# Latent attention: queries, keys and maxima from 4-byte pairs to scaled fp16 pairs

## The chip, the cores and the metric

The kernel runs on one core of a Trainium2 chip. The time is the device time of one execution in microseconds (us). Three runs were made, and their median is the time that counts.

## The reference

One encoder layer over 2048 tokens of width 1024: a first LayerNorm, a projection `w_in`, three groups of attention heads, a gate on each group's normalised output, an output projection and a closing LayerNorm. The change touches the second group, the latent attention of 8 heads. Cut to that:

```python
q = (_rms_norm(c_q, g_cq, dt) @ w_uq).reshape(b, s, MLA_HEADS, 64 + 32)
q_nope, q_rope = q[..., :64], _rope(q[..., 64:], pos)
kv = (_rms_norm(c_kv, g_ckv, dt) @ w_ukv).reshape(b, s, MLA_HEADS, 64 + 64)
k_nope, v = kv[..., :64], kv[..., 64:]
k_rope = _rope(b_kr[:, :, None, :], pos)[:, :, 0]          # one for all heads
sc = (einsum('bqhe,bkhe->bhqk', q_nope, k_nope)
      + einsum('bqhr,bkr->bhqk', q_rope, k_rope)) * 96 ** -0.5
o = einsum('bhqk,bkhe->bqhe', softmax(sc, axis=-1), v)
```

## The kernel before

**Split operands.** Products are made from a high and a low part of each operand: high by high, high by low and low by high, summed in PSUM. In the input projection both parts are fp16, scaled by a power of two that is worked out from the weights' norms (`Block.scale`, `root_power`). In the latent attention they are 4-byte parts in TensorE's fp32r form, without a scale (`R(...)` marks an operand so).

**Where the latent operands come from.** The last block of the projection, B_C + 3, gives the shared rotary key: in four chunks of 512 tokens it is scaled, turned and stored as `krh_d` and `krl_d` (lines 1160 to 1180). Then the pool `up` opens. `all_weights` loads `w_uq` in three pieces and `w_ukv` in two, and splits each on ScalarE and GpSimd; the first piece of `w_ukv` holds the keys, the second the values. The up-projection itself is cut into small steps (`up_chunk`: load, queries, rope, values, turn, keys), which stand in the list `fill`. The gate blocks 10 to 12 are projected meanwhile, and between two of their eight-part sums `paced(20, 1.4)` takes steps from `fill`: none in the first 20 calls (two and a half gate chunks), then 1.4 per call. `split_store` makes the two parts of 512 queries or keys, on ScalarE and VectorE (GpSimd for the rotary part), and stores them to `mqh_d`, `mql_d`, `mrh_d`, `mrl_d`, `mkh_d`, `mkl_d`. Its buffers, tags `uh` and `ul`, are also those of the raw weights.

**Order.** From the memory keys on, TensorE's instructions run in the order of the program (`in_order()`), while a planner orders the other engines and the DMA queue. From the dilated attention on, all engines run in the program's order (`in_order(*EALL)`).

**The latent attention.** A `Head` loads the four tiles `qh`, `ql`, `kh`, `kl` (96 rows of 2048) of its head, while the head before is worked on. Row 96 of `kh` is a constant and row 96 of `qh` holds the negated maximum of each query's scores, so that the first of the three products subtracts it. The maxima are made ahead, two steps per unit: a product of the high parts (`product`, line 1451), a reduction on VectorE (line 1457), and for each 512 queries a turn through TensorE and a conversion on ScalarE (`max_turn`, lines 1463 to 1468), whose result a DMA brings to row 96. A unit is 512 queries against 256 keys: six score matmuls (lines 1503 to 1505), two exponentials of the same 1024 columns on ScalarE (`probabilities`: `pf` in fp32, line 1349, and `ph` in fp16, line 1360), their difference `pl` on VectorE or, each third time, GpSimd (line 1363), and later 24 value matmuls (lines 1528 to 1530). `push_two` runs units in pairs: scores of both, then the value matmuls of two earlier units. The bias of the exponentials is `shift_t`, 4 ln 2. The dilated attention before it uses the same `probabilities` with a scale from a tile, `ascale`.

## Time and profile before

| | us |
|---|---|
| median of three runs | 2882.62 |
| lowest and highest | 2881.8, 2887.9 |
| the profiled execution, its own time | 2884.62 |
| its span in the profile | 2882.9 |
| TensorE busy | 2713.0 (94%) |
| VectorE busy | 1959.8 (68%) |
| ScalarE busy | 1547.0 (54%) |
| GpSimd busy | 929.1 (32%) |

In the profile PE is TensorE's matmul, PEld its weight load, DVE is VectorE, ACT ScalarE, POOL GpSimd and SP the engine that issues the DMAs; L12 is line 12 of the kernel. Matmuls are pipelined: a matmul's duration runs to the modelled end of its results, and the next starts before that. The profiled execution's own time is 1.7 us over its span.

### The profile page before, as it was taken

What the parts mean: (1) busy time and instruction counts of PE and PEld (TensorE: products, weight loads), DVE (VectorE), ACT (ScalarE), POOL (GpSimd) and SP (SyncE); (2) the same over time, 40 slices, a digit from 0 to 9 for tenths busy, and PEclk for the clock granted to TensorE, in tenths of its full rate; (3) what the DMA queues carried; (4) which work ended last, traced back from release to release, by engine and by line L of the source; (5) the groups of instructions that cost most, each with busy time, mean ns of one, the idle gap of its engine ahead of it and who ended that gap; (6) DMA issues with size and microseconds to landing.
All of it is one profiled execution on the core that took longest, in us unless ns stands there. A gap on an engine that the chain in (4) does not pass through costs nothing. (4 is left out here: it accounts for less than half of the span.)

```text
span 2882.9 us, 56842 instructions
## 1 busy us (share of the span) xinstructions
PE 2713.0 (94%) x22618; PEld 1893.3 (66%) x22665; DVE 1959.8 (68%) x4483; ACT 1547.0 (54%) x2071; POOL 929.1 (32%) x628
## 2 busy tenths in 40 slices
PE   6999999999999999899888888999999999899998
PEld 5544445544546774454777776888888877778887
DVE  7433344469982776543788887777777778688886
ACT  7644435532124665342788885878887767422221
POOL 3101013433232001212777773333333335222221
PEclk9999999999999999999999999999999999999999
DMA  5434346653224112686578596312323312556662
GB/s 179 140 102 131 97 143 152 167 154 102 83 79 150 54 54 93 204 276 213 149 167 209 155 185 138 75 33 75 82 66 68 70 41 64 158 167 176 180 181 90
DMA packets 279337, 367.53 MB, mean 127 GB/s; under 512 B 38304, under 2 KB 198176, under 8 KB 274976
## 3 DMA queue, kind: packets, MB, share of 16 engines
q1 hardware_dynamic: 279072, 363.90, 46.3%
q8 instruction: 178, 2.92, 0.4%
q14 instruction: 87, 0.71, 0.1%
HBM read 225.57 MB, written 138.20 MB: 126 GB/s over the span
## 5 line engine op out<-in xcount | busy, mean ns | idle before, releaser
L181 PE MATMUL ps_mm<-hT,w_h 128*128 128x512 f16 x2944 | 879.3, 381 | 4.6 <-ACT w_h L338 4.6
L181 PE MATMUL ps_mm<-hT,w_l 128*128 128x512 f16 x1472 | 558.0, 380 | 0.4 <-DVE w_l L342 0.4
L181 PEld LDWEIGHTS <-w_h 128*128 128x128 f16 x2944 | 277.2, 99 | 283.4 <-issue 20.5
L1363 POOL TENSOR_TENSOR pl<-pf,ph 128x1024 f16<-128x1024 f32 x117 | 297.7, 2544 | 465.1 <-ACT ph L1360 306.4
L1457 DVE TENSOR_REDUCE lmc<-ps_x 128x1 f32<-128x512 f32 x496 | 319.2, 685 | 143.1 <-PE ps_x L1451 142.6
L1349 ACT ACTIVATE pf<-ps_s,shift_t 128x1024 f32<-128x1024 f32 x256 | 285.5, 1115 | 138.1 <-PE ps_s L1505 134.3
L1363 DVE TENSOR_TENSOR pl<-pf,ph 128x1024 f16<-128x1024 f32 x217 | 292.4, 1348 | 7.3 <-ACT ph L1360 6.2
L1360 ACT ACTIVATE ph<-ps_s,shift_t 128x1024 f16<-128x1024 f32 x254 | 282.7, 1113 | 0.0
L181 PEld LDWEIGHTS <-w_l 128*128 128x128 f16 x1472 | 144.5, 98 | 175.3 <-DVE w_l L342 1.5
L1349 ACT ACTIVATE pf<-ps_s,shift_t,ascale 128x1024 f32<-128x1024 f32 x160 | 192.7, 1204 | 83.2 <-PE ps_s L1701 46.9
L1503 PE MATMUL ps_s<-hq,hq 97*128 97x512 f32 x512 | 218.7, 427 | 13.4 <-DMA hq<-lmr 11.2
L1528 PEld LDWEIGHTS <-ph 128*128 128x128 f16 x2032 | 187.4, 97 | 33.6 <-issue 33.1
L1530 PE MATMUL ps_o<-lv,pl 128*128 128x65 f16 x2032 | 202.1, 193 | 3.7 <-POOL pl L1363 3.7
L1504 PE MATMUL ps_s<-hq,hq 96*128 96x512 f32 x512 | 205.0, 400 | 0.0
L1528 PE MATMUL ps_o<-lv,ph 128*128 128x65 f16 x2032 | 204.1, 194 | 0.0
L1505 PE MATMUL ps_s<-hq,hq 96*128 96x512 f32 x512 | 203.6, 398 | 0.0
L1529 PE MATMUL ps_o<-lv,ph 128*128 128x64 f16 x2032 | 202.9, 196 | 0.0
L1530 PEld LDWEIGHTS <-pl 128*128 128x128 f16 x2032 | 189.3, 100 | 4.1 <-POOL pl L1363 3.8
L1529 PEld LDWEIGHTS <-ph 128*128 128x128 f16 x2032 | 189.4, 98 | 0.0
L1701 PE MATMUL ps_s<-hq,hq 128*128 128x256 f16 (+3 forms) x1536 | 185.6, 258 | 2.8 <-issue 0.2
L880 DVE CUSTOM_DVE_ANT_0 d1j<-ps_x,wm 128x256 bf16<-128x256 f32 (+1 forms) x608 | 184.7, 364 | 1.6 <-PE ps_x L877 0.8
L1701 PEld LDWEIGHTS <-hq 128*128 128x128 f16 (+1 forms) x1536 | 149.4, 120 | 39.5 <-issue 10.5
(379 smaller groups left out, 6086.4 us busy)
## 6 DMA issues: line engine op xcount, KB each, us to landing
w_raw<-in_w_in_dram SPq DMA_DIRECT2D x56, 512.0 KB
oa<-oa_d SPq DMA_DIRECT2D x48, 520.0 KB
v<-va_d SPq DMA_DIRECT2D x24, 1032.0 KB
oa_d<-so SPq DMA_DIRECT2D x16, 1040.0 KB
gate_d<-sg SPq DMA_DIRECT2D x64, 256.0 KB
lv<-gate_d SPq DMA_DIRECT2D x15, 1024.0 KB
wo_raw<-in_w_out_dram SPq DMA_DIRECT2D x26, 512.0 KB
hq<-k_n SPq DMA_DIRECT2D x16, 576.0 KB
```

What stands on the lines that cost most here:

```text
L181: nc.tensor.matmul(ps, R(a), R(b), start=(i == 0), stop=(i == n - 1))
L1349: nc.scalar.activation(pf, ps, AF.Exp, bias=shift_t, scale=scale)
L1360: nc.scalar.activation(ph, ps, AF.Exp, bias=shift_t, scale=scale)
L1363: pipe.later.append(lambda: lo_engine.tensor_tensor(out=pl, in0=pf, in1=ph, op=ALU.subtract))
L1457: nc.vector.tensor_reduce(out=self.mc[:, t % 4, n:n + 1], in_=ps, axis=AX.X, op=ALU.max)
L1503: nc.tensor.matmul(b, R(cur.kh[0:97, kc]), R(cur.qh[0:97, c]), start=True, stop=False)
L1504: nc.tensor.matmul(b, R(cur.kh[0:96, kc]), R(cur.ql[0:96, c]), start=False, stop=False)
L1505: nc.tensor.matmul(b, R(cur.kl[0:96, kc]), R(cur.qh[0:96, c]), start=False, stop=True)
L1528: nc.tensor.matmul(o, ph, v[:, 0:65], start=(k2 == 0 and j == 0 and i == 0), stop=False, skip_group_check=True)
L1529: nc.tensor.matmul(o[:, 0:64], ph, v[:, 65:129], start=False, stop=False, skip_group_check=True)
L1530: nc.tensor.matmul(o, pl, v[:, 0:65], start=False, stop=(k2 == 7 and j == 1 and i == 3), skip_group_check=True)
L1701: nc.tensor.matmul(o, kt[:, key], q, start=(i in bare and kt is ks and first), stop=(kt is kk and c0 == 512), skip_group_check=True)
```

## The change

The latent queries, keys, rotary keys and negated maxima become fp16, in the scratch memory and on the chip (`head_set(..., F16)` for both sets). To fit them into fp16's range, powers of two are worked out on the chip from the norms of the gain-weighted up-projection weights: `squares_of` sums squares of the raw weights on ScalarE, and `latent_powers` adds them over the partitions with a matmul and takes roots and products on VectorE. The queries and keys are multiplied by their power as they are split; the rotary key is left in its block's scale. The exponent's scale undoes the powers, from a tile, and the shift of 4 ln 2 moves from the exponential's bias into the row of maxima. `split_store` has buffers of its own. `root_power` can guard against zero.

```diff
-    mqh_d = scratch("mqh_d", [BH, 64, S])
+    mqh_d = scratch("mqh_d", [BH, 64, S], F16)
...
+    lpow = cpool.tile([P, 3], F32, name="lpow")
+    lscale = cpool.tile([P, 2], F32, name="lscale")
+    krinv = cpool.tile([P, 1], F32, name="krinv")
...
-        def root_power(dst, src):
-
-            y = wpool.tile([P, 1], F32, tag="rp", name="rp")
+        def root_power(dst, src, guard=False):
+
+            y = wpool.tile([P, src.shape[-1]], F32, tag="rp", name="rp")
+            if guard:
+                nc.vector.tensor_scalar(out=y, in0=src, scalar1=1e-20, scalar2=None, op0=ALU.max)
+                src = y[:]
             nc.vector.tensor_scalar(out=y.bitcast(I32), in0=src.bitcast(I32), scalar1=-0.5, scalar2=float(0x5F3759DF + (14 << 23)),
...
-                root_power(self.ws[:], ps[:, 8:9])
+                root_power(self.ws[:], ps[:, 8:9], self.b == B_C + 3)
...
-                nc.vector.tensor_tensor(out=sg, in0=sg, in1=w.un, op=ALU.mult)
+
+                nc.vector.tensor_scalar(out=sg, in0=sg, scalar1=2.0 ** -14, scalar2=None, op0=ALU.mult)
+                nc.vector.tensor_scalar(out=krinv, in0=w.un, scalar1=2.0 ** 14, scalar2=None, op0=ALU.mult)
...
-                    nc.vector.scalar_tensor_tensor(out=t1, in0=ps[0:32, :], scalar=w.un[0:32, :], in1=tb[0][0:32, :], op0=ALU.mult, op1=ALU.mult)
+                    nc.vector.scalar_tensor_tensor(out=t1, in0=ps[0:32, :], scalar=2.0 ** -14, in1=tb[0][0:32, :], op0=ALU.mult, op1=ALU.mult)
...
-                    kh = kr.tile([32, 512], F32, tag="k4", bufs=1, name="kh")
-                    nc.scalar.copy(R(kh[:]), t1)
-                    kl = kr.tile([32, 512], F32, tag="k5", bufs=1, name="kl")
-                    nc.vector.tensor_tensor(out=R(kl[:]), in0=t1, in1=kh, op=ALU.subtract)
+                    kh = kr.tile([32, 512], F16, tag="k4", bufs=1, name="kh")
+                    nc.scalar.copy(kh, t1)
+                    kl = kr.tile([32, 512], F16, tag="k5", bufs=1, name="kl")
+                    nc.vector.tensor_tensor(out=kl, in0=t1, in1=kh, op=ALU.subtract)
...
         with tc.tile_pool(name="up", bufs=2, side="right", reuse_waits="tile") as up:
+            gains = up.tile([P, 3], F32, bufs=1, name="gains")
+            nc.sync.dma_start(out=gains[:, 0:2], in_=g_cqT)
+            nc.sync.dma_start(out=gains[:, 2:3], in_=g_ckvT)
+            fros = up.tile([P, 7], F32, bufs=1, name="fros")
+
+            def squares_of(raw, name, b):
+
+                if name == "wk" and b:
+                    return
+                for i in range(2 if name == "wq" else 1):
+                    v = raw[:, :, i * P:(i + 1) * P]
+                    junk = up.tile([P, 512], BF16, tag="fj", bufs=1, name="fj")[:, 0:v.shape[1] * P].rearrange("p (b f) -> p b f", f=P)
+                    k = b + i if name == "wq" else 6
+                    nc.scalar.activation(junk, v, AF.Square, scale=gains[:, (i if name == "wq" else 2):(i if name == "wq" else 2) + 1],
+                                         accum_out=fros[:, k:k + 1])
+
+            def latent_powers():
+
+
+                t = up.tile([P, 3, 3], F32, bufs=1, name="lp_t")
+                for i, (a, b) in enumerate(((0, 4), (4, 6), (6, 7))):
+                    nc.vector.tensor_reduce(out=t[:, 0, i:i + 1], in_=fros[:, a:b], axis=AX.X, op=ALU.add)
+                ps = ps_x()
+                nc.tensor.matmul(ps[:, 0:3], ones_f, t[:, 0, :], start=True, stop=True)
+                root_power(t[:, 1, :], ps[:, 0:3], True)
+                p = t[:, 1, :]
+                nc.vector.tensor_scalar(out=p, in0=p, scalar1=2.0 ** -4, scalar2=None, op0=ALU.mult)
+                q = t[:, 2, :]
+                nc.vector.tensor_tensor(out=q[:, 0:1], in0=p[:, 0:1], in1=p[:, 2:3], op=ALU.mult)
+                nc.vector.reciprocal(q[:, 2:3], krinv)
+                nc.vector.tensor_tensor(out=q[:, 1:2], in0=p[:, 1:2], in1=q[:, 2:3], op=ALU.mult)
+                nc.vector.tensor_tensor(out=q[:, 2:3], in0=q[:, 0:1], in1=q[:, 1:2], op=ALU.min)
+                nc.vector.reciprocal(q[:, 0:1], p[:, 2:3])
+                nc.vector.tensor_copy(lpow[:, 2:3], p[:, 2:3])
+                nc.vector.tensor_tensor(out=lpow[:, 0:1], in0=q[:, 2:3], in1=q[:, 0:1], op=ALU.mult)
+                nc.vector.tensor_tensor(out=lpow[:, 1:2], in0=q[:, 2:3], in1=krinv, op=ALU.mult)
+                nc.vector.tensor_scalar(out=lscale[:, 1:2], in0=q[:, 2:3], scalar1=SHIFT * 96 ** 0.5 / ONE, scalar2=None, op0=ALU.mult)
+                nc.vector.reciprocal(q[:, 0:1], q[:, 2:3])
+                nc.vector.tensor_scalar(out=lscale[:, 0:1], in0=q[:, 0:1], scalar1=96 ** -0.5, scalar2=None, op0=ALU.mult)
...
@@ -1224,6 +1273,7 @@
...
                     nc.sync.dma_start(out=raw, in_=src[part].rearrange("b p n -> p b n"))
+                    squares_of(raw, name, b)
                     nc.scalar.copy(R(hi[:, part, :]), raw)
...
             wqh, wql = all_weights(w_uq, 256, 6, "wq")
             wkh, wkl = all_weights(w_ukv, 128, 8, "wk")
+            latent_powers()
...
-            def split_store(src, dh, dl, engine):
-                h = up.tile([P, 512], F32, tag="uh", name="uh")
-                nc.scalar.copy(R(h[:]), src)
-                lo = up.tile([P, 512], F32, tag="ul", name="ul")
-                engine.tensor_tensor(out=R(lo[:]), in0=src, in1=h, op=ALU.subtract)
+            def split_store(src, dh, dl, power=None):
+                h = up.tile([P, 512], F16, tag="sh", name="sh")
+                lo = up.tile([P, 512], F16, tag="sl", name="sl")
+                if power is None:
+                    nc.scalar.copy(h, src)
+                    nc.gpsimd.tensor_tensor(out=lo, in0=src, in1=h, op=ALU.subtract)
+                else:
+                    nc.scalar.activation(h, src, AF.Copy, scale=power)
+                    nc.vector.scalar_tensor_tensor(out=lo, in0=src, scalar=power, in1=h, op0=ALU.mult, op1=ALU.subtract)
                 nc.sync.dma_start(out=dh, in_=h)
                 nc.sync.dma_start(out=dl, in_=lo)
...
-                        nc.vector.tensor_tensor(out=t1, in0=first, in1=tb[:, 0, :], op=ALU.mult)
+                        nc.vector.scalar_tensor_tensor(out=t1, in0=first, scalar=lpow[:, 1:2], in1=tb[:, 0, :], op0=ALU.mult, op1=ALU.mult)
                         t2 = up.tile([P, 512], F32, tag="ul", name="u2")
-                        nc.vector.tensor_tensor(out=t2, in0=other, in1=tb[:, 1, :], op=ALU.mult)
+                        nc.vector.scalar_tensor_tensor(out=t2, in0=other, scalar=lpow[:, 1:2], in1=tb[:, 1, :], op0=ALU.mult, op1=ALU.mult)
                         nc.gpsimd.tensor_tensor(out=t1, in0=t1, in1=t2, op=op)
-                        split_store(t1[:], mrh_d[half, :, c], mrl_d[half, :, c], nc.gpsimd)
+                        split_store(t1[:], mrh_d[half, :, c], mrl_d[half, :, c])
...
+    def probabilities(pool, ps, scale, lo_engine, hi_engine=None, bufs=(4, 6), pair=None, select=None, bias=shift_t):
...
-        nc.scalar.activation(pf, ps, AF.Exp, bias=shift_t, scale=scale)
+        nc.scalar.activation(pf, ps, AF.Exp, bias=bias, scale=scale)
...
-            nc.gpsimd.memset(self.kh[96:97, :], 1.0)
+            nc.gpsimd.memset(self.kh[96:97, :], ONE)
...
-            mr = hq.tile([4, P], F32, tag="lmr", name="lmr")
-            nc.scalar.activation(R(mr[:]), pt[0:4, 0:P], AF.Copy, scale=-1.0)
+            mr = hq.tile([4, P], F16, tag="lmr", name="lmr")
+            nc.scalar.activation(mr, pt[0:4, 0:P], AF.Identity, scale=-1.0 / ONE, bias=lscale[0:4, 1:2])
...
-                    return lambda: probabilities(da, ps, 96 ** -0.5, lo_eng(), pair=early_pairs[k2])
-                return lambda: probabilities(la, ps, 96 ** -0.5, lo_eng(), bufs=(3, 5))
+                    return lambda: probabilities(da, ps, lscale[:, 0:1], lo_eng(), pair=early_pairs[k2], bias=0.0)
+                return lambda: probabilities(la, ps, lscale[:, 0:1], lo_eng(), bufs=(3, 5), bias=0.0)
...
+                msets[0] = head_set(m0.enter_context(tc.tile_pool(name="m0", bufs=1, side="right", reuse_waits="tile")), 0, F16)
...
```

## Rows read from the trace of the kernel before

**Rows 1.** Stages: busy us (instructions) by engine, granted clock, DMA share, GB/s.

```profile
1177.00:1327.00 150.00, 135.34 (x683) 79.27 (x682) 67.07 (x119) 61.76 (x101) 29.07 (x22) 0.99 0.83 259
1938.00:2208.00 270.00, 270.00 (x3230) 223.07 (x3230) 212.09 (x307) 217.16 (x223) 94.21 (x38) 1.00 0.31 74
```

**Rows 2.** Groups by shape, TensorE, latent scores: busy us, mean ns | idle before.

```profile
L1503 PE MATMUL ps_s<-hq,hq 97*128 97x512 f32 x512 | 218.7, 427 | 13.4 <-DMA hq<-lmr 11.2 <-ACT ph L1360 2.0
...
L1451 PE MATMUL ps_x<-hq,hq 96*128 96x512 f32 x496 | 159.0, 399 | 10.4 <-DVE lmc L1457 10.1
...
L1504 PEld LDWEIGHTS ps_s<-hq,hq 96*128 96x128 f32 x512 | 99.0, 193 | 15.4
```

**Rows 3.** Waits of TensorE, 1758 to 2475: total us, times, longest.

```profile
PE ps_s L1503 <- DMA hq<-lmr: 11.2, 3, 6.1
PE ps_x L1451 <- DVE lmc L1457: 10.1, 5, 5.8
```

**Rows 4.** Timeline of TensorE, a pair of latent units: start us, us.

```profile
2101.19 0.21 PE L1528 MATMUL ps_o<-lv,ph 128*128 128x65 f16 x1
...
2102.67 0.48 PE L1503 MATMUL ps_s<-hq,hq 97*128 97x512 f32 x1
2102.99 0.40 PE L1504 MATMUL ps_s<-hq,hq 96*128 96x512 f32 x1
...
2104.62 0.40 PE L1503 MATMUL ps_s<-hq,hq 97*128 97x512 f32 x1
...
2106.02 0.61 PE L1451 MATMUL ps_x<-hq,hq 96*128 96x512 f32 x2
```

**Rows 5.** Timeline of TensorE, gate projections (24 steps from first to last).

```profile
600.52 0.38 PE L181 MATMUL ps_mm<-hT,w_l 128*128 128x512 f16 x1
...
605.70 0.38 PE L181 MATMUL ps_mm<-hT,w_l 128*128 128x512 f16 x1
```

**Rows 6.** Groups by shape, ScalarE: pointers and accumulator reads.

```profile
L1349 ACT ACTIVATE pf<-ps_s,shift_t 128x1024 f32<-128x1024 f32 x256 | 285.5, 1115 | 138.1 <-PE ps_s L1505 134.3 <-PE ps_x L1451 3.0
...
L1349 ACT ACTIVATE pf<-ps_s,shift_t,ascale 128x1024 f32<-128x1024 f32 x160 | 192.7, 1204 | 83.2 <-PE ps_s L1701 46.9 <-PE ps_o L1372 33.9 <-POOL pf L1643 0.5
...
L1130 ACT ACTIVATE sq<-ps_mm,un 128x512 f32<-128x512 f32 x12 | 8.2, 682 | 0.0
...
L323 ACT ACTIVATION_READ_ACCUMULATOR w_l<-w_raw 128x1 f32 x40 | 7.7, 191 | 0.0
```

**Rows 7.** Timeline of ScalarE and the DMA queue, start of the up-projection.

```profile
1182.08 1.47 SPq L1226 DMA_DIRECT2D w_raw<-in_w_uq_dram  x3
1182.52 0.69 ACT L738 ACTIVATE sg<-ps_mm,un 128x512 f32<-128x512 f32 x1 [0.23 <-PE ps_mm L181]
...
1188.01 0.63 SPq L1226 DMA_DIRECT2D w_raw<-in_w_ukv_dram  x1
...
1189.15 0.62 ACT L1227 CAST wkh<-w_raw 128x512 fp32r<-128x512 f32 x1 [1.14 <-DMA w_raw<-in_w_ukv_dram]
...
1198.29 0.62 ACT L1227 CAST wkh<-w_raw 128x512 fp32r<-128x512 f32 x1 [6.89 <-DMA w_raw<-in_w_ukv_dram]
```

**Rows 8.** Queue, TensorE and stages around the first head's second row of maxima.

```profile
1769.38 1.85 SPq L1435 DMA_DIRECT2D hq<-mqh_d  x1
...
1780.23 0.66 SPq L1468 DMA_DIRECT2D hq<-lmr  x1
...
1790.04 0.77 PE L1503 MATMUL ps_s<-hq,hq 97*128 97x512 f32 x1 [6.11 <-DMA hq<-lmr]
...
1782.00:1786.00 4.00, 1.93 (x49) 1.64 (x49) 2.42 (x3) 2.04 (x3) 0.00 (x0) 1.00 1.01 205
1790.00:1794.00 4.00, 3.96 (x9) 3.14 (x10) 0.60 (x1) 0.97 (x1) 0.00 (x0) 0.50 0.11 41
```

**Rows 9.** Waits of TensorE, 1177 to 1327: total us, times, longest.

```profile
PE ps_x L181 <- DVE ul L1242: 7.7, 5, 2.1
...
PE ps_x L181 <- DMA cq<-cql_d: 1.6, 1, 1.6
```

More of the change, by code (lines that the diff above doesn't have):

```diff
@@ L114, in tile_layer @@
     ckl_d = scratch("ckl_d", [P, S])
-    mqh_d = scratch("mqh_d", [BH, 64, S])
-    mql_d = scratch("mql_d", [BH, 64, S])
-    mrh_d = scratch("mrh_d", [2, P, S])
-    mrl_d = scratch("mrl_d", [2, P, S])
-    mkh_d = scratch("mkh_d", [BH, 64, S])
-    mkl_d = scratch("mkl_d", [BH, 64, S])
-    krh_d = scratch("krh_d", [32, S])
-    krl_d = scratch("krl_d", [32, S])
+    mqh_d = scratch("mqh_d", [BH, 64, S], F16)
+    mql_d = scratch("mql_d", [BH, 64, S], F16)
+    mrh_d = scratch("mrh_d", [2, P, S], F16)
+    mrl_d = scratch("mrl_d", [2, P, S], F16)
+    mkh_d = scratch("mkh_d", [BH, 64, S], F16)
+    mkl_d = scratch("mkl_d", [BH, 64, S], F16)
+    krh_d = scratch("krh_d", [32, S], F16)
+    krl_d = scratch("krl_d", [32, S], F16)
     vb_d = scratch("vb_d", [BH // 2, S, 258], F16)
@@ L399, in token_bound @@
             nc.vector.tensor_scalar(out=hbound, in0=t[:, 3:4], scalar1=2.0, scalar2=None, op0=ALU.mult)
-            root_power(hs[:, 0:1], hbound[:])
+            root_power(hs[:, 0:1], hbound[:], True)
             nc.vector.reciprocal(hs[:, 1:2], hs[:, 0:1])
@@ L1275, in queries @@
                 def queries(b):
-                    split_store(up_q(b)[:], mqh_d[2 * b:2 * b + 2, :, c], mql_d[2 * b:2 * b + 2, :, c], nc.vector)
+                    split_store(up_q(b)[:], mqh_d[2 * b:2 * b + 2, :, c], mql_d[2 * b:2 * b + 2, :, c], lpow[:, 0:1])
                 def keys(b):
-                    split_store(up_kv(b)[:], mkh_d[2 * b:2 * b + 2, :, c], mkl_d[2 * b:2 * b + 2, :, c], nc.vector)
+                    split_store(up_kv(b)[:], mkh_d[2 * b:2 * b + 2, :, c], mkl_d[2 * b:2 * b + 2, :, c], lpow[:, 2:3])
                 def rope(which):
@@ L1345, in tile_layer @@
     W2 = 1024
-    def probabilities(pool, ps, scale, lo_engine, hi_engine=None, bufs=(4, 6), pair=None, select=None):
+    def probabilities(pool, ps, scale, lo_engine, hi_engine=None, bufs=(4, 6), pair=None, select=None, bias=shift_t):
         pf = pool.tile([P, W2], F32, tag="pf", bufs=bufs[0], name="pf")
-        nc.scalar.activation(pf, ps, AF.Exp, bias=shift_t, scale=scale)
+        nc.scalar.activation(pf, ps, AF.Exp, bias=bias, scale=scale)
         ph, pl = pair or [pool.tile([P, W2], F16, tag=tag, bufs=bufs[1], name=tag) for tag in ("ph", "pl")]
@@ L1359, in probabilities @@
         elif hi_engine is None:
-            nc.scalar.activation(ph, ps, AF.Exp, bias=shift_t, scale=scale)
+            nc.scalar.activation(ph, ps, AF.Exp, bias=bias, scale=scale)
         else:
@@ L1803, in all_units @@
                 lv.extend(lvp.tile([P, NT * 258], F16, name=f"lv{i}") for i in range(2))
-                msets[0] = head_set(m0.enter_context(tc.tile_pool(name="m0", bufs=1, side="right", reuse_waits="tile")))
+                msets[0] = head_set(m0.enter_context(tc.tile_pool(name="m0", bufs=1, side="right", reuse_waits="tile")), 0, F16)
                 head = Head(0)
@@ L1982, in tile_layer @@
         la = la_pool.enter_context(tc.tile_pool(name="la", bufs=2, reuse_waits="tile"))
-        msets[1] = head_set(m1.enter_context(tc.tile_pool(name="m1", bufs=1, reuse_waits="tile")))
+        msets[1] = head_set(m1.enter_context(tc.tile_pool(name="m1", bufs=1, reuse_waits="tile")), 0, F16)
         w0, waiting = [], []
```

## The prediction

> **What bounds the kernel now.** I began with the page: TensorE is busy 94% of the span, and its share hardly moves over the 40 slices. So I cut the span into the stages that the change touches [rows 1]. In the latent attention (one undisturbed stretch of 270 us) TensorE is busy for all of it, at the full 2.4 GHz; VectorE has 212 us of work there and ScalarE 217 us. In the up-projection (1177 to 1327 us) TensorE is still busy 135 of 150 us, while the DMA engines are at 83%, the highest of any stage I cut. TensorE's rows [rows 2] then say what a latent score costs and how often it is run: lines 1503 to 1505 have 512 matmuls each, and the product for the maxima (line 1451) 496: 2032 matmuls of 512 columns in all on 4-byte operands, each with a weight load of 193 ns. What the reader should see is that the latent stage has one limit: TensorE's waits in all of it [rows 3] are 23 us of some 715. A shorter matmul there shortens the kernel one for one, until VectorE or ScalarE is full.
>
> **The change, part by part.**
>
> *Score matmuls on fp16 operands.* A matmul's own duration overlaps its neighbours, so I take the distance of starts. In the timeline [rows 4] six score matmuls, from the start at 2104.62 to the one at 2106.02, take 1.40 us: 0.233 us each. Fp16 matmuls of the same 512 columns in the gate projections [rows 5] take 24 steps from 600.52 to 605.70: 0.216 each. Saved: 0.0175 x 2032 = 35.6 us. The trace has no fp16 matmul of 512 columns over 96 or 97 rows, so the bounds are 0 and this value; I take this value, since the fp16 row is the nearest. There is also a switch cost: after the 48 short value matmuls the first score starts at 2102.67 and the next at 2102.99, 0.32 instead of 0.233. The 4-byte weight load of 193 ns is too long to hide behind matmuls some 30 ns apart; an fp16 load should hide. There are 256 units in pairs, 128 such switches, each worth up to 0.085: another 10 us. Bounds 0 and 11. Together 46 us.
>
> *Does another engine fill up?* One pair of units holds 16 such matmuls and 48 short ones (1.48 us from 2101.19 to 2102.67): 16 x 0.233 + 1.48 + 0.09 = 5.29 now, 16 x 0.216 + 1.48 = 4.94 after. By their busy time [rows 1] VectorE has 212/270 x 5.29 = 4.16 per pair, ScalarE 4.25. Both stay under 4.94, VectorE at 84%. Its reductions already hold TensorE now and then (10.1 us in all [rows 3], 5.8 of them once in the last head). I charge 3 us for more of this.
>
> *Exponentials.* They now take their scale from a pointer, and their bias is a constant 0 instead of the pointer shift_t. With pointers for both, as in the dilated stage, the instruction takes 1204 ns; with one, 1115 [rows 6]. The squares of line 1130 have a pointer scale and no stated bias and take 682 ns for 512 elements, in line with one pointer. So I take 1115, unchanged. The Trainium skill (ScalarE: Activation LUTs, What ACT_TABLE_LOAD costs) says that each pointer operand adds about 93 ns; these rows agree, with 89 between them. By that rule, an estimate, a constant 0 that is itself kept behind a pointer would add 93 x 4 = 0.37 us per pair. With the rows' 89, ScalarE's pair would be 4.61, still below 4.94: a cost, but not on the path.
>
> *The new wait: latent_powers.* TensorE's order is the program's, and the new matmul of ones_f with the sums stands behind the last key projection and ahead of all gate chunks. It needs the squares of the raw weights. Before, those loads lay behind 13 us of gate projections; now the projections are queued behind them. The first gate chunk's SiLU starts at 1182.52 [rows 7]; the chunk takes 5.18 [rows 5], so TensorE is free for the new matmul at about 1177.1. The weights are issued at 1182.08, and the fourth, the last needed, is in use at 1189.15. Two small loads of gains ahead cost about 1 us on the queue. ScalarE then has, for each of three w_uq tiles, two squares of 256 elements (about 0.47 each by the slope between the 1024- and 512-element rows, plus 0.19 for reading the accumulator [rows 6]) and the old 0.62 copy: 5.8 us from 1186.1; then one square of 512 (0.87): 1192.8. With the sums and the weight load TensorE goes on at 1193.3: a stall of 16 us. After a wait of 6.1 us elsewhere the granted clock stood at 0.50 for the next 4 us [rows 8]: 2 us of work lost, and some more until it is back; I add 2.5. Bounds: 5 us if the weights arrive as soon as TensorE is free, and 67 in the rival below.
>
> *The up-projection itself.* Stores are half as large and have buffers of their own instead of sharing uh and ul with the raw weights. TensorE waited 7.7 us there on ul and 1.6 on the latents' first load [rows 9]. The second vanishes behind the stall; I take 5 of the first: 7 us back. Bounds 1.6 and 14.6 (all idle time there). The evictions gain a pointer (about 0.1 us, 32 times) on engines that are busy under half of this stage: nothing on the path, at most 3 us uncovered. The extra tiny VectorE instructions (a guard, powers, some twenty at about 0.15) run while TensorE waits, or 13 us before the first query needs them.
>
> *Head loads.* A head's ten loads bring 3.1 MB (192 rows of 2048, high and low, 4 bytes), now 1.6. The row of maxima queues behind them: issued at 1780.23, it is there only at 1790.04, and TensorE idles 6.1 us [rows 8]; three such waits make 11.2 us [rows 3]. With 1.6 MB less ahead at the 205 GB/s of that stretch, 8 us, the long ones nearly go: 9 us, and 4 for the clock after them (0.50 granted for 4 us is 2, twice). Bounds 0 and 16. The row's own conversion, with one pointer more, is 0.1 us, 31 times, beside TensorE's work. The halved memset on GpSimd lies beside other work too.
>
> *Sum.* The profiled execution took 2884.6 us (span 2882.9): 2884.6 - 46 + 3 + 16 + 2.5 - 7 - 9 - 4 = 2840. It was 2 us above the median, so I predict **2838** for the median.
>
> **Rivals.**
>
> *The stall is hidden* (0.13). If the weight loads are issued before the key stage's last stores (for memory, they need only buffers that may be free earlier), the 16 + 2.5 goes to a few us: 2838 - 15 = 2823. Against it: the loads of before left right behind those stores.
>
> *VectorE or ScalarE becomes the pace* (0.15). The averages leave 0.7 us, but each waits in order, and two subtractions can fall in one pair. If half of the 46 is lost in waits on reductions or exponentials: 2861. Against it: the first exponentials of the units waited 138 us, nearly all of it for TensorE's scores [rows 6].
>
> *The scores get no faster* (0.06). If 0.233 is not set by the 4-byte weight load, only the loads and stores gain: 2838 + 46 - 3 = 2881, no change. Against: fp16 rows at 0.216 with the same columns.
>
> *Slower: the weights come late* (0.06). The stall at latent_powers is one for one. One of the five weight loads, issued at 1188.01, was in use only at 1198.29 [rows 7], 10.3 us later. Should all needed ones come one behind another at that price, with the gains, the stall is near 67: 2838 + 51 = 2889. It decides once the stall passes 16 + 44 = 60 us.
>
> **How the numbers follow.** Forecast 0.60, the rivals 0.13, 0.15, 0.06 and 0.06. The forecast's own range is 2827 to 2850. The range given, 2822 to 2860, takes in the first rival and nearly all of the second. Faster by over 0.2% (below 2877; about what a measurement here can tell from no change): 0.60 + 0.13 + 0.15 = 0.88; within it 0.06; slower 0.06.
>
> **What would show it.** Score starts 0.216 apart at the full clock and pairs of 4.9 to 5.0 us; no 0.32 step behind the value matmuls; exponentials still at about 1115 ns; a wait of some 16 us of TensorE on the new matmul at about 1177, with a granted clock of half behind it; waits on the row of maxima of 2 us or less instead of 11. I am wrong if the pair stays above 5.1, if exponentials of 1200 hold TensorE, or if the stall is far from 16.

## The result, and the profile after

The changed kernel takes 2854.65 us in the median (four runs, 2847.24 to 2866.82), the kernel before 2882.21 in the same measurement: a ratio of 0.9901, with a 95% interval of 0.9883 to 0.9919. It is faster, inside the stated range of 2822 to 2860, and 17 us above the point of 2838. It also lies above the forecast's own range of 2827 to 2850, toward the rival in which VectorE or ScalarE becomes the pace (2861). The profiled execution took 2855.82 us, 28.8 less than that of before, where the sum expected 44.6 less.

First the stages, by windows (us and instructions of TensorE, weight loads, VectorE, ScalarE, GpSimd; granted clock, DMA share, GB/s). They answer to [rows 1], taken 15 and 12 us later, since the work stands later.

```profile
1192.00:1342.00 150.00, 138.63 (x683) 81.50 (x684) 69.30 (x129) 62.91 (x101) 24.99 (x20) 0.95 0.60 177
1950.00:2220.00 270.00, 269.38 (x3470) 163.69 (x3469) 226.27 (x331) 231.87 (x236) 97.16 (x39) 1.00 0.18 47
```

In the same 270 us of latent attention there are now 3470 matmuls instead of 3230, 7.4% more, and TensorE is still busy nearly all the time (269.4 us). VectorE has gone from 212 to 226 us of them, ScalarE from 217 to 232: closer to full, as the sum of one pair said. In the up-projection the DMA share falls from 0.83 to 0.60.

The groups of TensorE and of its weight loads in the latent stage, by shape (busy us, mean ns, idle before), answer to [rows 2].

```profile
L1558 PE MATMUL ps_s<-hq,hq 97*128 97x512 f16 x512 | 196.9, 385 | 7.0 <-DMA hq<-lmr 4.1 <-ACT ph L1415 2.9
...
L1506 PE MATMUL ps_x<-hq,hq 96*128 96x512 f16 x496 | 152.9, 381 | 16.5 <-DVE lmc L1512 15.2 <-ACT lmr L1522 0.7
```

```profile
L1559 PEld LDWEIGHTS <-hq 96*128 96x128 f16 x512 | 50.7, 99 | 46.2 <-issue 4.7
```

The weight load is 99 ns instead of 193. What counts is the distance of starts, in TensorE's timeline of one pair of units, as in [rows 4].

```profile
2104.36 0.38 PE L1558 MATMUL ps_s<-hq,hq 97*128 97x512 f16 x1
2104.57 0.38 PE L1559 MATMUL ps_s<-hq,hq 96*128 96x512 f16 x1
...
2105.66 0.59 PE L1506 MATMUL ps_x<-hq,hq 96*128 96x512 f16 x2
...
2109.30 0.38 PE L1558 MATMUL ps_s<-hq,hq 97*128 97x512 f16 x1
```

From 2104.36 to 2105.66 there are six steps of 0.217 us; the first one behind the short value matmuls is 0.21 and not 0.32; the pair takes 2109.30 - 2104.36 = 4.94 us, which was the figure worked out beforehand.

TensorE's waits in the latent stage (total, times, longest) answer to [rows 3]. The wait on the row of maxima fell from 11.2 to 4.1 us; the wait on VectorE's reductions rose from 10.1 to 15.2.

```profile
PE ps_x L1506 <- DVE lmc L1512: 15.2, 12, 6.1
PE ps_s L1558 <- DMA hq<-lmr: 4.1, 2, 3.0
PE ps_s L1558 <- ACT ph L1415: 2.9, 3, 1.4
```

The new matmul in the timeline, with the end of what it waits for, and the granted clock by windows around it:

```profile
1187.56 0.51 ACT L1242 ACTIVATE fj<-w_raw,gains 128x256 bf16<-128x256 f32 x1 [5.17 <-DMA w_raw<-in_w_uq_dram]
...
1193.99 0.19 ACT L1242 ACTIVATION_READ_ACCUMULATOR fj<-w_raw,gains 128x1 f32 x1
1194.21 0.15 DVE L1250 TENSOR_REDUCE lp_t<-fros 128x1 f32<-128x1 f32 x1 [0.69 <-ACT fj L1242]
...
1194.42 0.59 PE L1252 MATMUL ps_x<-lp_t,ones_f 128*128 128x3 f32 x2 [16.18 <-DVE lp_t L1250]
```

```profile
1186.00:1190.00 4.00, 0.00 (x0) 0.00 (x0) 0.00 (x0) 2.38 (x7) 1.26 (x2) 0.50 0.92 291
...
1194.00:1198.00 4.00, 3.58 (x10) 1.61 (x11) 1.92 (x15) 0.17 (x2) 0.00 (x0) 0.50 0.88 223
1198.00:1202.00 4.00, 4.00 (x16) 1.58 (x14) 0.00 (x0) 1.90 (x2) 1.26 (x1) 0.77 0.08 30
```

TensorE waits 16.18 us, and afterwards has the lower of its two clock levels (1.2 GHz) until some point between 1198 and 1202. The trace puts that point at 1199.9: 5.4 us at half clock behind the restart, 2.7 us of work lost.

**Where the time went.** The conversion of a row of maxima on ScalarE happens once every four pairs of units, 32 times, so the distances of these conversions cut the latent stage into 31 stretches. "Start" is the first score of the stage, "3-25" the mean of these stretches. The columns behind the first two are for the experiments; "best" is the run with both edits that helped.

```
                before   after   4-byte  loads x2  wol out  low on VectorE  best
start          1758.57 1772.70  1779.87   1770.21  1772.69      1775.27  1760.57
stretch 1        22.80   23.54    22.84     22.10    22.11        22.11    22.11
stretch 2        30.61   20.82    30.88     29.74    20.82        20.81    20.83
3-25 (mean)      21.35   20.01    21.29     20.00    20.00        20.00    20.32
stretch 26       31.57   29.75    32.23     27.97    29.39        29.57    28.37
27-31 (sum)     115.61  115.93   115.14    115.39   105.95       124.80   102.93
```

The stage starts 14.1 us later. Its regular stretches are 1.34 us shorter each, 31 times that is 41.6. Stretch 2 gives 8.5 us beyond that; stretches 27 to 31 give nothing at all and so lose 7.0 of it; the first stretch loses 2.1 of it. From its first score to its last the stage is 41.6 us shorter, and the tail behind it 1.3.

Part of this is TensorE's clock. Windows over stretch 1 of the changed kernel and of the best version, then over stretch 30 of the kernel before and of the changed one:

```profile
1770.60:1794.10 23.50, 19.59 (x229) 11.73 (x228) 20.95 (x28) 15.33 (x16) 7.62 (x4) 0.93 0.63 152
1758.30:1780.50 22.20, 18.63 (x235) 11.32 (x234) 21.03 (x28) 15.36 (x17) 5.96 (x3) 1.00 0.40 97
2396.40:2417.70 21.30, 21.30 (x258) 17.62 (x257) 17.81 (x25) 16.80 (x18) 12.39 (x5) 1.00 0.30 87
2366.20:2389.60 23.40, 21.69 (x258) 13.19 (x257) 19.53 (x25) 16.91 (x18) 12.32 (x5) 0.93 0.27 85
```

Stretch 1 takes 23.5 us in the profiles where its granted clock is 0.93, and 22.1 where it is 1.00, with nearly the same three waits in it (1.2, 1.7 and 1.1 us against 0.9, 1.6 and 1.1). Stretch 26 goes from 26.4 us (0.94) to 29.8 (0.84) in profiles whose edits do not touch it, and stretches 27 to 31 together from 113.6 to 115.9. So 1.4 of the 2.1 us of stretch 1, and about half of the 7.0 of the last heads (by the granted clock 6.7 us are lost there, 3.4 in the kernel before), are half clock. Why the clock falls in one execution and not in another with the same waits is not shown.

### The profile page after: what moved, and what is told of

The parts are those of the page before. It is cut to its first block, busy times and chain, and to the rows that moved or that the text cites. A ratio compares the mean times of both kernels' runs of the same rounds, so it can differ in the third digit from the quotient of the medians.

```text
span 2854.1 us, 56720 instructions
## 1 busy us (share of the span) xinstructions
PE 2679.6 (94%) x22667; PEld 1719.7 (60%) x22667; DVE 1952.4 (68%) x4504; ACT 1556.6 (55%) x2085; POOL 929.2 (33%) x628
## 4 chain that ended last, share of the span: by engine, by line
PE 43%; DVE 11%; ACT 4%; POOL 3%; issue 3%; DMA 3%; SPq 0%; DVEq 0%; POOLq 0%; ACTq 0%
PE ps_s L2031 10%; PE ps_mm L185 7%; PE ps_s L1559 3%; PE ps_s L1558 3%; PE ps_x L1506 3%; PE ps_s L1560 3%; PE ps_x L185 2%; DVE pl L1412 2%; PE ps_o L1584 2%; PE ps_o L1585 2%; PE ps_o L1583 2%; ACT pf L1404 2%; DVE pl L1418 1%; POOL pl L1418 1%; POOL pf L1698 1%
## 5 line engine op out<-in xcount | busy, mean ns | idle before, releaser
L1404 ACT ACTIVATE pf<-ps_s,lscale 128x1024 f32<-128x1024 f32 x256 | 285.0, 1113 | 100.4 <-PE ps_s L1560 99.4
L1415 ACT ACTIVATE ph<-ps_s,lscale 128x1024 f16<-128x1024 f32 x254 | 282.7, 1113 | 0.1
L1558 PE MATMUL ps_s<-hq,hq 97*128 97x512 f16 x512 | 196.9, 385 | 7.0 <-DMA hq<-lmr 4.1
L1559 PE MATMUL ps_s<-hq,hq 96*128 96x512 f16 x512 | 196.7, 384 | 0.0
L1560 PE MATMUL ps_s<-hq,hq 96*128 96x512 f16 x512 | 195.3, 381 | 0.0
L1756 PEld LDWEIGHTS <-hq 128*128 128x128 f16 (+1 forms) x1536 | 149.2, 120 | 39.8 <-issue 10.1
```

The source lines that it names most:

```text
L1404: nc.scalar.activation(pf, ps, AF.Exp, bias=bias, scale=scale)
L1415: nc.scalar.activation(ph, ps, AF.Exp, bias=bias, scale=scale)
L1558: nc.tensor.matmul(b, R(cur.kh[0:97, kc]), R(cur.qh[0:97, c]), start=True, stop=False)
L1559: nc.tensor.matmul(b, R(cur.kh[0:96, kc]), R(cur.ql[0:96, c]), start=False, stop=False)
L1756: nc.tensor.matmul(o, kt[:, key], q, start=(i in bare and kt is ks and first), stop=(kt is kk and c0 == 512), skip_group_check=True)
```

## The experiments

Three things were to be settled: what the wait of 16 us really costs; whether the time that the stretches miss is ScalarE, loads or VectorE; and whether the gain is the operands' size and nothing else. Each run had the kernel before beside it, and its ratio is to that. Differences to the changed kernel are between medians, with its 2854.38 us of the next paragraph.

**The changed kernel again**, without an edit.

> The changed kernel itself, unaltered, beside the runs of this series. Both theories below are counted from its time here. The first measurement gave a median of 2854.65 us; I expect 2848 to 2860.

2854.38 us (2847.81 to 2861.13), ratio 0.99 (0.9884 to 0.9916). Its profile repeats stretches 2 to 25 to 0.01 us; of the stretches, only 26 to 31 move, by 2.8 us together.

**latent_powers later.**

```diff
-            latent_powers()
...
             fill.popleft()()
+            fill[2] = latent_powers
```

> Only the place of latent_powers changes: it is called as the third step of the up-projection's fill, behind a part of the first gate chunk, instead of ahead of it. Theory A (the 16.2 us that TensorE waits on the sums of squares is exposed only because nothing stands behind it in TensorE's order): TensorE runs gate matmuls meanwhile, the wait on lp_t falls under 2 us, the half clock after it goes, the wait on the first latents (1.6 us) may come back; 14 to 19 us faster than the changed kernel, about 2838. Rival B (the weights are late in any case, and the first query projection waits for them and for the powers instead): the wait moves to the query's first matmul or to the eviction, and less than 5 us is gained.

2842.3 us (2837.92 to 2843.13), ratio 0.9854 (0.9841 to 0.9868): 12.1 us less. TensorE's wait on the sums, in the list of its waits:

```profile
PE ps_x L1252 <- DVE lp_t L1250: 3.8, 1, 3.8
```

Theory A holds in its mechanism, not in its numbers (14 to 19 us, a wait under 2): 3.8 us of wait are left, and TensorE's clock is at 0.50 once more from 1198 to 1202. Most of the stall was exposed only by its place in TensorE's order. Between the two profiled executions (13.3 us) the latent stage starts 9.4 us earlier; another 3.4 lie in stretch 26, which the edit does not touch (granted clock 0.94 for 0.84).

**Two pointers at the exponentials.**

```diff
-    lscale = cpool.tile([P, 2], F32, name="lscale")
+    lscale = cpool.tile([P, 3], F32, name="lscale")
+    nc.vector.memset(lscale[:, 2:3], 0.0)
...
-                return lambda: probabilities(la, ps, lscale[:, 0:1], lo_eng(), bufs=(3, 5), bias=0.0)
+                return lambda: probabilities(la, ps, lscale[:, 0:1], lo_eng(), bufs=(3, 5), bias=lscale[:, 2:3])
```

> The exponentials of the latent units take their bias of 0 from a tile instead of as a constant, so each has two pointers: about 1204 ns instead of 1113, 4 per pair of units, 0.36 us more of ScalarE's time per pair (4.25 to 4.6 of 4.94). Theory A (TensorE is the pace of the regular heads, ScalarE has the slack that the sum gave it): 0 to 6 us slower than the changed kernel, and the waits on ph and pf stay small. Rival B (ScalarE, working in order, is already the pace, which is why the scores gave 42 instead of 56 us): each of 128 pairs grows by up to 0.36 us, 20 to 45 us slower.

2856.73 us, ratio 0.9908 (0.9893 to 0.9923): 2.4 us more, inside the intervals. The exponentials, by shape over 270 us, do take longer:

```profile
L1405 ACT ACTIVATE pf<-ps_s,lscale 128x1024 f32<-128x1024 f32 x107 | 128.5, 1201 | 21.5 <-PE ps_s L1561 21.5
```

1201 ns against 1113, 0.35 us per pair, and the mean regular stretch grows by 0.14 us, not by 1.4. ScalarE is not the pace; rival B is out. The Trainium skill (ScalarE: Activation LUTs, What ACT_TABLE_LOAD costs) gives about 93 ns for a pointer; this run shows 88, and a constant bias of 0 next to a pointer scale ran at the one-pointer time.

**The first output block's loads later.**

```diff
-        for at, *fs in (((6, 0, 4), p.load, p.load_m, p.load_h), ((6, 0, 7), p.two), ((6, 1, 2), p.three), ((6, 1, 5), p.merge),
-                        ((6, 2, 2), p.load_gate), ((6, 2, 5), p.scale_a), ((7, 1, 4), p.load_b),
+        for at, *fs in (((6, 0, 7), p.load, p.load_m, p.load_h), ((6, 1, 3), p.two), ((6, 1, 6), p.three), ((6, 2, 1), p.merge),
+                        ((6, 2, 4), p.load_gate), ((6, 2, 7), p.scale_a), ((7, 1, 4), p.load_b),
```

> In the seventh latent head the three loads for the first output block (oa, om, h; 1.8 MB) and the steps that use them are planned three units later, so that the row of maxima is on SP's queue ahead of them and not behind them. Theory A (the one long wait on the row of maxima that is left, 2.96 us and the half clock after it, stands behind these loads and not behind the head's own loads): the wait at 2282 us goes, 5 to 9 us faster than the changed kernel. Rival B (it stands behind the next head's loads, or the loads held back collide with the following row of maxima): the wait stays or moves by one block, within 2 us of the changed kernel.

2854.89 us, ratio 0.9899 (0.9884 to 0.9914): no difference. In the changed kernel the queue's timeline has the row of maxima behind these loads, and TensorE's shows the wait:

```profile
2270.64 0.65 SPq L1935 DMA_DIRECT2D oa<-oa_d  x1
...
2272.30 0.59 SPq L1940 DMA_DIRECT2D ht<-h_d  x1
2275.53 0.63 SPq L1523 DMA_DIRECT2D hq<-lmr  x1
```

```profile
2282.36 0.59 PE L1558 MATMUL ps_s<-hq,hq 97*128 97x512 f16 x1 [2.96 <-DMA hq<-lmr]
```

With the edit that wait is gone and stretch 26 falls from 29.75 to 23.65, so its cause was named rightly: these loads, not the head's own. But stretch 27, where the steps that use the loads now fall, rises from 20.87 to 24.43: two of VectorE's `pl` take 3.15 us in it, each begun while a GpSimd instruction ran (the runs on `wol` below show what that does), and the granted clock averages 0.93. Theory A was right on the wait and wrong on the gain.

**Powers kept, operands 4-byte again.**

```diff
-    mqh_d = scratch("mqh_d", [BH, 64, S], F16)
+    mqh_d = scratch("mqh_d", [BH, 64, S])
...
-                h = up.tile([P, 512], F16, tag="sh", name="sh")
+                h = up.tile([P, 512], F32, tag="uh", name="sh")
...
-        msets[1] = head_set(m1.enter_context(tc.tile_pool(name="m1", bufs=1, reuse_waits="tile")), 0, F16)
+        msets[1] = head_set(m1.enter_context(tc.tile_pool(name="m1", bufs=1, reuse_waits="tile")))
```

The seven other scratch tensors, `msets[0]`, `lo`, `kh`, `kl` and `mr` are changed in the same way, with their writes in the fp32r form; staging shares `uh` and `ul` with the raw weights again, and three small constants share one tile.

> The powers, the squares of the raw weights, the pointers and the shift in the row of maxima stay; operands, scratch, staging tiles and head tiles of the latent scores are 4-byte again (staging shares uh and ul with the raw weights, as before the change). Theory A (the gain is the fp16 matmul's shorter spacing, the hidden switch and the halved head loads; all the rest of the change is cost): the regular four-pair stretch goes back to about 21.2 us from 20.05, the wait of 6 us on the row of maxima at the start of the latent stage comes back, the 16 us wait on lp_t stays; 2898 to 2912, slower than the kernel before by 15 to 28 us. Rival B (part of the gain comes from something else in the change, such as the pointer forms or the shift folded away): below 2890.

2906.04 us, ratio 1.008 (1.0065 to 1.0095): slower than before by 21 us. That is theory A's range. Its column shows both halves of the account: the regular stretches are back at 21.29, stretch 2 at 30.88, and the stage starts 21.3 us later than before. All that makes the kernel faster is the operands' size, together with the staging buffers that it made room for; all the rest costs 21 us.

**Loads of a head twice** (the ten loads go first into four spare tiles).

```diff
+            if spare:
+                self.loads(h, spare)
+            self.loads(h, msets[h % 2])
```

> Each head's ten loads (from the second head on) are issued twice, first into spare tiles that nothing reads, so that a head's loads bring 3.1 MB again, ahead of the row of maxima on the queue; matmuls are those of the changed kernel. Theory A (halved loads took away the wait of 6.1 us on the row of maxima near the start of the stage, with the half clock behind it): the first stretch behind it grows from 20.8 to about 29 us, the last long wait grows too; 8 to 15 us slower than the changed kernel. Rival B (the waits were short because the stores or the alignment of the steps had changed, not for the bytes ahead): less than 3 us slower.

2860.23 us, ratio 0.9916 (0.9896 to 0.9936), about 5 us over the changed kernel; by the time alone the intervals overlap. The stretch decides it: stretch 2 is 29.74 again, 8.9 more, with this row in TensorE's timeline.

```profile
1801.20 0.58 PE L1565 MATMUL ps_s<-hq,hq 97*128 97x512 f16 x1 [6.34 <-DMA hq<-lmr]
```

So the halved loads took that wait away. The later wait did not grow (stretch 26: 27.97), in line with the run with later loads: it belongs to the first output block's. Theory A's 8 to 15 us were too many: stretches 1 and 26, at a higher clock in this profile, hide 3.2 of the 8.9 in the profiled execution.

**wol on VectorE.** In the last head eight tiles `wol`, the low parts of `w_out`, are made on GpSimd.

```diff
-                low(w0[0], waiting.pop(), nc.gpsimd)
+                low(w0[0], waiting.pop(), nc.vector)
```

> In the last latent head the eight subtractions for the low parts of w_out (wol) run on VectorE instead of GpSimd. In the changed kernel eight or nine VectorE instructions of that head take 1.7 to 3.2 us instead of 0.7 to 1.2, and each of them ends 1.08 us (two-input subtractions) or 0.02 us (the three-element ones) after a GpSimd instruction that had begun before it. Theory A (a GpSimd instruction that begins first holds VectorE's SBUF work until it ends; this is what ate the gain of the last two heads): with no wol on GpSimd the long ones fall to 1.2 us except where GpSimd's own share of the pl subtractions does it, VectorE gets 8 x 1.2 us more work, and the last head gets 2 to 6 us shorter. Rival B (VectorE is simply full in that head): 9.6 us more work make it 3 to 8 us longer.

2865.2 us, ratio 0.9935 (0.992 to 0.9951): about 10 us slower than the changed kernel. Theory A (2 to 6 us shorter) failed, and the time went the way of rival B, and past its 3 to 8 us. Yet the mechanism behind theory A is visible. First the changed kernel's last head, VectorE's timeline and then GpSimd's:

```profile
2373.13 1.77 DVE L1418 TENSOR_TENSOR pl<-pf,ph 128x1024 f16<-128x1024 f32 x1
...
2376.02 3.16 DVE L1418 TENSOR_TENSOR pl<-pf,ph 128x1024 f16<-128x1024 f32 x1
2379.11 2.47 DVE L1512 TENSOR_REDUCE lmc<-ps_x 128x1 f32<-128x512 f32 x4
2381.50 1.21 DVE L1418 TENSOR_TENSOR pl<-pf,ph 128x1024 f16<-128x1024 f32 x1
```

```profile
2371.39 2.42 POOL L1921 TENSOR_TENSOR wol<-wo_raw,woh 128x1024 fp32r<-128x1024 f32 x1
2375.97 2.13 POOL L1418 TENSOR_TENSOR pl<-pf,ph 128x1024 f16<-128x1024 f32 x1 [2.16 <-issue]
2378.07 3.38 POOL L1921 TENSOR_TENSOR wol<-wo_raw,woh 128x1024 fp32r<-128x1024 f32 x1
```

Undisturbed, VectorE's subtraction takes 1.21 us. The two long ones start after a GpSimd instruction has begun (2371.39, 2375.97), and end at 2374.90 and 2379.18, both 1.08 us after its end (2373.81, 2378.10). The reductions at 2379.11, which read PSUM, keep 0.6 to 0.7 us each while GpSimd runs. Counting each VectorE instruction of the latent stage that begins while a GpSimd instruction runs, ends after it and takes over 0.3 us more than the fastest of its kind, there are 14 in the changed kernel, drawn out by 19 us in all, and 13 with 18 us in that of before. So it is not that there are more of them: with shorter pairs TensorE waits for them. In stretches 30 and 31 its waits on VectorE's reductions are 9.9 us, where they were 5.8. Now the run with wol on VectorE, its VectorE and its GpSimd:

```profile
2373.19 1.21 DVE L1921 TENSOR_TENSOR wol<-wo_raw,woh 128x1024 fp32r<-128x1024 f32 x1
2374.33 3.15 DVE L1418 TENSOR_TENSOR pl<-pf,ph 128x1024 f16<-128x1024 f32 x1
```

```profile
2374.08 2.31 POOL L1418 TENSOR_TENSOR pl<-pf,ph 128x1024 f16<-128x1024 f32 x1 [10.11 <-ACT ph L1415]
```

VectorE is late by its wol, so GpSimd's own `pl` starts first, and VectorE's next one is held: six of these at 3.15 us. So the order in which the two start matters, beside who has how much work. How much of the 10 us is these holds, and how much the 9.7 us of work that VectorE got, this run does not separate. The Trainium skill (SBUF — State Buffer, SBUF: two separate sides) states this as a lock on a pair of ports, for VectorE instructions with two inputs in SBUF against GpSimd instructions that read SBUF: whichever starts first keeps the pair for its whole instruction, and the other blocks. The trace agrees: every held `pl` ends 1.08 to 1.09 us after GpSimd's instruction.

**wol left out.**

```diff
+            if engine is nc.gpsimd and c < 8:
+                nc.scalar.copy(R(wol[c][:]), raw)
+            else:
                 engine.tensor_tensor(out=R(wol[c][:]), in0=raw, in1=woh[c], op=ALU.subtract)
```

> The eight wol subtractions of the last latent head are left out: each tile is filled by a ScalarE copy of the raw weight (about 1.06 us each), so the output product has wrong low parts for eight blocks. Theory A (collisions with GpSimd): the last head's stretches fall toward 20 to 21 us per four pairs plus its preparations, 4 to 9 us faster than the changed kernel, more than the run with wol on VectorE. Rival B (the last head is held by the preparations of the first output block, not by wol): within 2 us of the changed kernel.

2843.02 us, ratio 0.9857 (0.9843 to 0.9872), 11.4 us under the changed kernel, more than theory A's 4 to 9; stretches 27 to 31 take 105.95 us instead of 115.93 (113.6 to 115.9 in the four profiles that leave the last head as it is). VectorE's `pl`, by shape in the last head:

```profile
L1418 DVE TENSOR_TENSOR pl<-pf,ph 128x1024 f16<-128x1024 f32 x26 | 31.7, 1219 | 3.9 <-ACT ph L1415 3.9
```

1219 ns in the mean, where the changed kernel has 1505 and the run with wol on VectorE 1679. That is the gain the last head did not show, and rival B is out.

**wol earlier.** The fp16 tiles freed 32 KB per partition, just the eight tiles.

```diff
-                        high(wo0, raws.pop())
+                        raw = raws.pop()
+                        high(wo0, raw)
+                        if len(wol) < 8:
+                            low(wo0, raw, nc.gpsimd)
...
-        plan((7, 0, 0), low_pool)
-        for i in range(9):
-            plan((7, 3 * i // 8, 3 * i % 8), next_low, i < 8)
+        plan((7, 0, 0), m0.close)
```

> The whole computation, with the eight wol subtractions moved from the last latent head to the heads 0 to 3, right behind the copies that make woh, while the raw weight is still there (their eight loads fall away; the 32 KB per partition are those that the fp16 head tiles freed). They stay on GpSimd. Theory A (in the last head VectorE's queue is loaded with the preparations, so a GpSimd instruction that holds it costs TensorE; in a regular head VectorE has 0.7 us of slack per pair and takes most of it): the last three stretches get 8 to 10 us shorter as they did with wol left out, the regular stretches with a wol grow by 0 to 0.6 us each, 4 to 10 us faster than the changed kernel. Rival B (a GpSimd instruction costs TensorE the same wherever it falls, about 1.2 us each): no gain, within 2 us of the changed kernel.

2850.17 us, ratio 0.9873 (0.9857 to 0.989). Stretches 27 to 31 give 11.8 us (104.17), three of the early stretches take 8.7 back (+3.4, +1.85, +3.4), where theory A allowed 0.6 each. VectorE's timeline and GpSimd's in the first of them:

```profile
1838.99 2.15 DVE L1418 TENSOR_TENSOR pl<-pf,ph 128x1024 f16<-128x1024 f32 x1
...
1842.27 2.93 DVE L1418 TENSOR_TENSOR pl<-pf,ph 128x1024 f16<-128x1024 f32 x1
```

```profile
1837.71 2.35 POOL L1924 TENSOR_TENSOR wol<-wo_raw,woh 128x1024 fp32r<-128x1024 f32 x1 [0.58 <-ACT woh L1919]
1841.99 2.13 POOL L1418 TENSOR_TENSOR pl<-pf,ph 128x1024 f16<-128x1024 f32 x1 [1.92 <-ACT ph L1415]
```

The wol holds one `pl`; VectorE is then late, GpSimd's own `pl` starts ahead of its next, and holds that too. Just the three stretches with two such holds in a row grow; three other wols hold a `pl` once, and their stretches cost nothing. The two that grew by 3.4 had a granted clock of 0.93, the one with 1.85 had 1.00. The gain is 4.2 us between medians and 7.8 by the ratios, and the interval alone does not part it from the changed kernel's.

**Both edits that helped.**

> The two edits that helped, together: wol made in the heads 0 to 3, and latent_powers called behind a part of the first gate chunk, one step later than when it was tried alone. Theory A (they act in different stages, so their gains add): 17 to 24 us faster than the changed kernel, 2831 to 2838; the wait of 3.8 us that was left on lp_t falls under 2. Rival B (the up-projection's later parts, not the stall, set when the latent stage starts, so the step later brings nothing or loses): 2839 to 2845.

2833.87 us (2833.06 to 2834.86), ratio 0.9823 (0.9808 to 0.9838): 1.8% under the kernel before and about 0.7% under the change as it was made, the best of all. The gains add, by the ratios (0.0046 and 0.0027 apart, 0.0077 together). The wait on the sums did not fall under 2 us, as theory A had it: it is 4.7, and the matmul starts at 1198.05 instead of 1197.52, though it stands a step later. What is late now is the sums, not the place.

**With the later loads too.**

> The two edits of the run before and the later loads for the first output block. Theory A (without wol in the last head, the VectorE work that the later loads push toward it has room, and the 6 us that the missing wait on the row of maxima gives are kept): 3 to 6 us faster than with the two edits. Rival B (the steps that use these loads collide with VectorE's subtractions in the next stretch whatever comes later, +3.6 us there as when it was tried alone): within 2 us of the two edits.

2840.21 us, ratio 0.9846 (0.9831 to 0.9861): 6 us worse, all four executions above those of the run before. Stretch 26 falls from 28.37 to 22.41, and the following five rise from 102.93 to 109.38, stretch 27 alone from 20.37 to 25.69. So in its own place the edit changes nothing (131.8 us for 131.3): theory A is out, and rival B holds there. Most of the profiled difference of 7.3 us lies ahead of the edit: 3.0 us at the start of the stage, 1.4 in stretch 1 and 1.5 in the stretches with held subtractions, with a lower granted clock over the execution (0.987 for 0.989). Why the clock is lower is not shown.

**wol early, on VectorE.**

```diff
-                            low(wo0, raw, nc.gpsimd)
+                            low(wo0, raw, nc.vector)
```

> As the version with both edits, but the eight wol subtractions of the heads 0 to 3 run on VectorE instead of GpSimd. With them on GpSimd, three stretches of those heads grew by 1.8 to 3.5 us, where a wol subtraction that had begun first held one of VectorE's for 2.0 to 2.2 us. Theory A (being held by GpSimd is what costs there; 1.2 us more of VectorE's own work fits into the 0.7 us of slack that each pair leaves): these three stretches fall back toward 19.7 to 21 us, 3 to 8 us faster than 2833.87. Rival B (VectorE has no room for any addition in one pair, whoever causes it): the stretches with a wol stay as long or more of them grow, no gain or up to 6 us slower.

2839.59 us, ratio 0.9856 (0.984 to 0.9872): worse again, by 5.7 us, and rival B's side of the forecast. Eight early stretches grow instead of three, the most by 4.0 us (24.15 for 20.16, at a granted clock of 0.93). Six of the eight have an instruction of VectorE that was held, four times a `pl` and twice the wol itself, and grow by 1.5 us or more; the two without one grow by 0.5. So VectorE has room for more than half of a wol's 1.23 us, and the hold costs more than the wol itself. VectorE's and GpSimd's timelines show the same turn of order:

```profile
1803.01 1.23 DVE L1924 TENSOR_TENSOR wol<-wo_raw,woh 128x1024 fp32r<-128x1024 f32 x1 [0.52 <-ACT woh L1919]
...
1805.35 3.16 DVE L1418 TENSOR_TENSOR pl<-pf,ph 128x1024 f16<-128x1024 f32 x1
```

```profile
1805.30 2.13 POOL L1418 TENSOR_TENSOR pl<-pf,ph 128x1024 f16<-128x1024 f32 x1 [5.37 <-ACT ph L1415]
```

A wol of 1.23 us on VectorE makes it 0.05 us late behind GpSimd, and that costs 1.9 us more.

## Why the prediction was right, point by point

**Scores on fp16 operands (-46): right in mechanism and in size.** Steps of 0.217, no switch cost, a pair of 4.94 us. The forecast was 46 - 3 = 43 over 32 stretches, 1.34 each; the regular ones gave 1.34. With 4-byte operands again, they are back at 21.29. Whether it is the weight load or the operand's width as such that sets 0.233 was not separated.

**VectorE and ScalarE (+3, and the rival that one of them becomes the pace): mis-sized.** For ScalarE the sum held: 0.35 us more per pair cost 0.04. For VectorE the average of 84% held in the regular heads and misled in the last: there it loses time to GpSimd's instructions, TensorE waits for it, and its clock falls with the waits. In the profiled execution stretches 27 to 31 gave 7 us less than the regular ones promise (5 to 7 in the four profiles that leave the last head as it is). wol left out gives 8 to 10 us there. This is the rival's place, but not the reason that it gave: neither two subtractions in one pair nor a full engine, but one held by another. The trace of before had 13 such instructions and could have told it.

**Exponentials (0): right**, 1113 ns for the 1115 of [rows 6].

**The stall (+16, +2.5): right.** 16.18 us, from a start of the squares that was 1.5 us later than worked out and an end that was 1.1 later, with TensorE free 1.1 us later too. The prediction's start of the squares, 1186.1, is the first copy of `w_uq` in the kernel before, and 1 us for the gains:

```profile
1185.07 1.22 ACT L1227 CAST wqh<-w_raw 128x512 fp32r<-128x512 f32 x2 [1.85 <-DMA w_raw<-in_w_uq_dram]
```

The clock behind it was at half for 5.4 us, so 2.7 us were lost where 2.5 had been added. Moved behind other work, most of the stall was given back: 12 us of the kernel's time, 9.4 us of it at the start of the latent stage.

**The up-projection (-7): right, as far as seen.** With 4-byte staging the latent stage starts at 1779.87, with fp16 between 1770.2 and 1775.3 in eight profiles that have the stall: 5 to 10 us. The stall itself was 18.2 us with 4-byte staging and 15.7 to 17.4 in the eight, so 1 to 2 us of it may not belong here.

**Waits on the row of maxima (-9, -4): right for the first, wrong for the last.** Stretch 2, that of the 6.1 us of [rows 8], gave 8.5 beyond its share (the granted clock over it went from 0.89 to 1.00), and gave it back when the loads were doubled. The wait in the seventh head stayed: I had put all long waits down to the head's own loads, and this one stood behind 1.8 MB for the first output block. 4 us of the 13 are missing here.

Together, in the profiled execution: 7.0 for the last heads, 4.1 for the wait that stayed, 2.1 for the first stretch (1.4 of it half clock), 1.4 of the rate (43 was for 32 stretches), 2.6 of the start, less 1.4 at the end of the stage and behind it: 15.8 us, the distance of 28.8 from 44.6. The misses nearly all point one way; the result is inside the stated range because that range took in the rival on VectorE, and outside the forecast's own.

## What to carry to other kernels

A matmul's price is the distance of starts in the stretch it runs in, and that gave the size of the gain in the regular stretches, 1.34 us each; what was lost lay in stretches of another make-up, so a gain per unit should be applied stretch by stretch, with a look at which stretches also carry other work. An engine at 84% is no reserve when another engine can hold it: look for its instructions that take far more than their usual time, and at what began just before them. A new dependence ahead of independent work costs its full latency, here 16 us of wait; the same dependence a few steps later, behind such work, left 3.8 us, and the kernel was 12 us faster.

## What the hardware showed that was not expected

VectorE's subtractions of two SBUF tiles wait for a GpSimd instruction that began first, and a lead of 0.05 us (1805.30 against 1805.35) is enough to make 1.21 us into 3.16. So taking work from GpSimd to VectorE, which looks like relief, cost 10 us in the last head and 6 in the first ones.
